# Key tiles of a gated DeltaNet's input in three products of rounded parts, S5 tables spawned one tile later, and a last norm with its sums in three banks

## The chip, the cores and the metric

The kernel runs on one core of a Trainium2 chip. The metric is the device time of one execution in microseconds (us); less is better. All weights lie in HBM in fp32, and every output is fp32.

## The reference, cut to what matters

One inference step of a trunk of four layers, for one prompt of 256 tokens and eight sample sequences of four tokens. Layers 0 and 3 mix with S5, layer 1 with RG-LRU, layer 2 with a gated DeltaNet (gdn); each is followed by a ConvFFN, and one norm ends the trunk. Left out are states, convolutions and the S5 and LRU bodies.

```python
for i in range(DEPTH):
    kind, j = i % N_MIXERS, i // N_MIXERS
    xn = rmsnorm(x, p['norm_mix'][i])
    ...
    x = x + y
    xn = rmsnorm(x, p['norm_ffn'][i])
    y, buf = conv_ffn(xn, ffn_conv[i], ...)
    x = x + y
x = rmsnorm(x, p['norm_final'])

def gdn_mixer(x, s0, conv_buf, w_in, conv_w, a_log, dt_bias, norm_w, w_out):
    proj = x @ w_in
    qkv, z, a_in, b_in = jnp.split(proj, ...)
    qkv, new_buf = causal_dwconv(qkv, conv_buf, conv_w)
    qkv = jax.nn.silu(qkv)
    ...
    beta = jax.nn.sigmoid(b_in)
    g = -jnp.exp(a_log) * jax.nn.softplus(a_in + dt_bias)
    o, s_last = chunked_gated_delta(q, k, v, g, beta, s0)
    o = rmsnorm(o, norm_w) * jax.nn.silu(z)
    return o @ w_out, s_last, new_buf
```

## The kernel before, in words

The 32 sample columns and the 256 prompt columns stand side by side as T = 288 columns of one activation tile `x` (128 partitions x 8 blocks of D = 1024). A projection goes output tile by output tile: `gemm` takes the weight tile of 128 outputs (`wr`, 512 KB, loaded by SP, four buffers) and issues one product of 128x128 weights with 128x288 activations per block of the contraction.

**Two ways of a product.** A weight tile is "whole" (`whole`, line 493) and multiplied in fp32 as it is, `wr` by `xh`; the profile shows two records for each such product. Or it is cut: `wh` is the tile rounded to fp32r (a copy on ACT or DVE), `wl` is the rest, `wr` minus `wh` (DVE or POOL), the activations are cut likewise into `xh` and `xl`, and `part` issues three products, `wh` by `xh`, `wh` by `xl` and `wl` by `xh`. The tiles of the gdn's input (`gdn_in`) are all whole before the change; those of the ConvFFN, the gdn's output and the S5's GLU are cut, with activations `gh` and `gl` there.

**The norm.** A sublayer's projection starts on the `x` that is not yet normed. Meanwhile the squares (`sm`, `acc`) are summed over partitions by products with ones (`busy`), one value for each column in a bank's three columns; twelve short DVE instructions (`nv`, `rsi`, `rst`, `rsr`) make the inverse root, two more a diagonal (`dg`), a product spreads it over all partitions, and DVE copies it from PSUM as `rstd`. Whoever evacuates a tile multiplies by `rstd`.

**Order.** A planner (`Net`) records all instructions at build time. It keeps a clock for each engine with prices and latencies of its own, holds tasks (generators) sorted by rank, and lets a task issue its next instructions when its clock says they are ready; where the TensorE would wait for the operand of a started tile it issues products with `busy` that nobody reads, to keep that engine occupied. The order on each engine is fixed by that, and engines wait for each other by semaphores. So an edit in one stage can move instructions in another.

**The gdn** (`gdn`, line 1529) does 32 tiles of eight products: keys 0 to 7, queries, values, queries, values, then the gates z. `scalars` multiplies the 16 columns of weights for a and b (`wab`) by `xh` and goes on with many short DVE operations to the decay. `ktile` and the like evacuate a tile (`ext`), convolve it (`cv`), apply silu (`kq`) and transpose it on TensorE (`ktm`); `gram`, `rows` and `inverse` build the triangular inverse of each chunk (`fh`, `inv`); `sample`, `update` (`s`), `prompt` and `heads` do the recurrences, with `tm` the normed and gated result of some heads, cut into `gh` and `gl` for the output projection.

**The other places.** `ffn` takes other tasks in `beside`: the tables of the S5 of layer 3 (`s5_tables`, some 200 short DVE instructions, names `er`, `ek`, `dt`, `ang`, `ee`) run beside the ConvFFN of layer 2 (`ffn_down2`). `final` (line 2274) is the last norm: `norm_rstd`, then eight times `y` = x by gain by `rstd` and a store each, with four buffers of `y`.

In the profile every recorded instruction has line 235, that of the planner's helper, and every load or store line 360; so rows are told apart by names. PSUM banks are `ps` and `px`.

Of the kernel before, what the change touches and what calls it, by code (L numbers as in the profile page):

```python
# [9 lines left out]
F32 = mybir.dt.float32  # L10
F32R = mybir.dt.float32r
I32 = mybir.dt.int32
AF = mybir.ActivationFunctionType
ALU = mybir.AluOpType
PSUM = bass.MemoryType.PSUM

P = 128
D = 1024
KD = D // P
NB, NT = 8, 4  # L20
NS = NB * NT
SEQ = 256
T = NS + SEQ
# [3 lines left out]
KL = LW // P  # L27
BLK = (slice(NS, NS + P), slice(NS + P, T), slice(0, P))
EPS = 1e-6
# [6 lines left out]
TR = 0, 0  # L36
HJ = 2
OE, CE = 0, 'a'
PRS, DB, TH, BI = 1, 4, 8, 0.0
SR, SS = (0, 2, 1), (1000.0, 2000.0)  # L40
WHOLE = (0, 4, 6)
WARM = 3500.0


# [248 lines left out]
class Net:  # L293
# [55 lines left out]
    def fresh(self, gi):  # L349

        kinds = (("xh", F32),) if gi in WHOLE else (("xh", F32R), ("xl", F32R)) if gi < 8 else ()
        self.xh, self.xl = ([self.xs.tile([P, KD, T], dt, name=n, tag=n) for n, dt in kinds] + [None, None])[:2]
# [140 lines left out]
    def whole(self, u):  # L493

        name, m = self.units[u][:2]
        return name.startswith(("s5_in", "gdn_in")) or name == "lru_in" and m >= KL

    def freed(self, u):
        return (self.over if self.whole(u) else self.cutl) > u
# [108 lines left out]
    def norm_tile(self, m, gi):  # L608
# [9 lines left out]
        if m == KD - 1:  # L618

            self.last = sq  # L620
            self.mark(("n", gi, m))
        if gi in WHOLE:
            self.mark(("x", gi, m))
        yield
        if gi < 8 and gi not in WHOLE:
            self.v.scalar_tensor_tensor(
# [90 lines left out]
    def ffn(self, li, gi, beside=()):  # L717
        tc, V, G, A = self.tc, self.v, self.g, self.act
        H = 2
        g0 = 2 * li + 1  # L720
        NE = NB * (H + NT) + H + SEQ
        NC = NE - H
        with ExitStack() as es:
            c = es.enter_context(tc.tile_pool(name="ffc", bufs=1))
# [54 lines left out]
            start, name = 2, f"ffn_up{li}"  # L779
            for m, ps in enumerate(self.gemm(name, range(start), KD, self.xh, self.xl, self.xready(g0))):  # L780
                self.spawn(up(m % 2, m // 2, ps))
            for m in range(start, 2 * KF):
                self.spawn(up(m % 2, m // 2, *self.gemm(name, [m], KD, self.xh, self.xl)))
            for g in beside:
                self.spawn(g)
            self.fresh(gi)
            for m in range(KD):
                ready = None if m else (lambda k: self.marked(("d", li, k)))
                self.spawn(self.residual(m, *self.gemm(f"ffn_down{li}", [m], KF, gh, gl, ready), gi))
                if m == 0:  # L790
                    self.dma(self.o["ffn_st"][li], sto)

    def exp_ops(self, p, x, pool, tag):

        V = self.v
        def t(n, dt=F32):
            return pool.tile(list(x.shape), dt, name=n, tag=f"{tag}{n}", bufs=1)
        xc, kf, r, s = t("ex"), t("ek"), t("er"), t("es", I32)
        V.tensor_scalar(xc, x, -87.0, 88.0, op0=ALU.max, op1=ALU.min)
        yield  # L800
        V.tensor_scalar(kf, xc, 1.0 / math.log(2.0), MAGIC + 127.0, op0=ALU.mult, op1=ALU.add)
        yield
        V.tensor_single_scalar(s, kf.bitcast(I32), 23, op=ALU.logical_shift_left)
        V.tensor_scalar_sub(kf, kf, MAGIC + 127.0)
        yield
        V.scalar_tensor_tensor(r, kf, -0.693145751953125, xc, op0=ALU.mult, op1=ALU.add)
        yield
        V.scalar_tensor_tensor(r, kf, -1.42860682030941723e-06, r, op0=ALU.mult, op1=ALU.add)
        yield
        yield from self.horner_ops(p, r, [1.0 / math.factorial(n) for n in range(8, 0, -1)])  # L810
        V.scalar_tensor_tensor(p, p, 1.0, s.bitcast(F32), op0=ALU.add, op1=ALU.mult)
        yield
# [716 lines left out]
    def gdn(self, gi):  # L1529
        tc, V, G, A, PE = self.tc, self.v, self.g, self.act, self.pe  # L1530
        NH, NTL = 8, 16
        H = 3
        g0 = 4
        NE = NB * (H + NT) + H + SEQ
        NC = NE - H
        with ExitStack() as es:
            c = es.enter_context(tc.tile_pool(name="gdc", bufs=1))
            def ct(n, shape, dt=F32):
                return c.tile(shape, dt, name=n)
# [5 lines left out]
            wab, dtp, gnorm = ct("wab", [P, KD, 16]), ct("dtp", [P, 2, NH]), ct("gnorm", [P, 1])  # L1545
# [18 lines left out]
            wh, wl = ct("wh", [P, P], F32R), ct("wl", [P, P], F32R)  # L1564
# [22 lines left out]
            x, xt = (t[:, :512].rearrange("p (t c) -> p t c", t=NTL) for t in inv)  # L1587
# [7 lines left out]
            def pack(dst, src):  # L1595
                for h in range(4):
                    V.tensor_copy(pk[32 * h : 32 * h + 32, dst, :], src[0:32, 2, h::4])

            def scalars():
                yield from self.after("gw")  # L1600
                ps = yield from self.banks.get()
                for k in range(KD):
                    yield from self.after(("x", g0, k))
                    PE.matmul(ps[0:16, :T], wab[:, k, :], self.xh[:, k, :], start=k == 0, stop=k == KD - 1)
                    if k % 2:
                        yield PE
                yield
                t = yield from tms.get()
                self.copy(t[0:16], ps[0:16, :T])
# [2 lines left out]
                ps = yield from self.banks.get()  # L1612
# [41 lines left out]
                ps, pd = yield from self.banks.get(2)  # L1654
# [7 lines left out]
                for h in range(NH):  # L1662
# [4 lines left out]
                        start=True, stop=True, tile_position=(0, 32 * q),  # L1667
# [5 lines left out]
                for hg in range(2):  # L1673
                    V.tensor_scalar(
                        ats[:, hg, :], pd[:, 32 * hg : 32 * hg + 32], pk[:, 0, hg : hg + 1], 0.0,
                        op0=ALU.subtract, op1=ALU.min,
# [554 lines left out]
            start = 2  # L2231
            tiles = self.gdn_order()

            self.spawn(self.norm_rstd(g0))
            self.spawn(scalars())
            self.spawn(sample(0), rank=RK[7])
            self.spawn(sample(1), rank=RK[7])
            fns = ktile, qtile, vtile, ztile
            def rk(m):
                return RK[(0, 0, 1, 3, 2, 4, 5, 5)[m // 4]]  # L2240
            for m, ps in zip(tiles, self.gemm("gdn_in", tiles[:start], KD, self.xh, self.xl, self.xready(g0))):
                self.spawn(fns[m // NH](m % NH, ps), rank=rk(m))
            for m in tiles[start:]:
                self.spawn(fns[m // NH](m % NH, *self.gemm("gdn_in", [m], KD, self.xh, self.xl)), rank=rk(m))
                if m == NH - 1:
                    for r in range(4):
                        self.spawn(gram(r), rank=RK[0])
                    self.spawn(kscalars(), rank=RK[0])
                    self.spawn(rows(), rank=RK[0])
                    self.spawn(inverse(0), rank=RK[0])  # L2250
                    self.spawn(inverse(1), rank=RK[0])
                elif m in (19, 23):
                    self.spawn(prompt((m - 19) // 4), rank=RK[6])
            self.spawn(finals())
            pss = self.gemm("gdn_out", (0, 1), KD, gh, gl, lambda k: self.marked(("gp", k), ("gs", k // 4)))
# [16 lines left out]
            self.ahead()  # L2272

    def final(self):
        self.drain()
        self.spawn(self.norm_rstd(8))
        self.drain()
        yp = self.ctx.enter_context(self.tc.tile_pool(name="yp", bufs=4))
        for m in range(KD):
            y = yp.tile([P, T], F32, name="y", tag="y")  # L2280
            self.v.scalar_tensor_tensor(
                y, self.x[:, m, :], self.gains[:, 8, m : m + 1], self.rstd, op0=ALU.mult, op1=ALU.mult
            )
            self.dma(self.o["y"][:, m, :], y)


def wtiles(w):
# [189 lines left out]
```

## Time and profile before

| | |
|---|---|
| runs | 1572.19, 1572.41, 1567.34 us; median 1572.19 |
| the profiled execution | 1569.18 us, its span 1567.4 us |
| mean granted TensorE clock | 0.98 of full speed |
| TensorE busy | 1503.2 us, 96% of the span |
| VectorE (DVE) busy | 1280.4 us, 82% |
| ScalarE (ACT) busy | 807.0 us, 51% |
| GpSimd (POOL) busy | 360.8 us, 23% |

The span runs from the first to the last instruction of the profiled execution, which is one of its own beside the three runs. Matmuls are pipelined: consecutive records of one stream overlap, so a product's cost is the distance between starts. A row of a timeline gives start, duration, engine, line, operation, out<-in, shapes and count, with the idle time ahead of it and the instruction that ended it in square brackets.

### The profile page before, as it was taken

Reading aid. Unit: us, or ns where it says so; the run is one execution under the profiler, and the core shown is the slowest. Engines: PE = TensorE matmul, PEld = TensorE weight load, DVE = VectorE, ACT = ScalarE, POOL = GpSimd, SP = SyncE. Lnnn points to the kernel's source line nnn. Section 1 sums busy time; section 2 is a strip of 40 time slices with the busy share of each in tenths; the row PEclk is TensorE's granted clock in tenths of the full one; section 3 lists DMA queues with packets and bytes.
Section 4 is the critical chain, followed back from the end, with each engine's and each line's share of the span. In section 5 each row is a group of like instructions: output and inputs, shape, how many; then the busy total and the mean of one; then the engine's idle time right before and its main releaser. Section 6 shows DMA issues by size and latency. Waiting matters only on the chain. (4 is left out here: it accounts for less than half of the span.)

```text
span 1567.4 us, 32702 instructions
## 1 busy us (share of the span) xinstructions
PE 1503.2 (96%) x12527; PEld 1390.6 (89%) x12527; DVE 1280.4 (82%) x2884; ACT 807.0 (51%) x1594; POOL 360.8 (23%) x734
## 2 busy tenths in 40 slices
PE   6689999999999999999999999999999899999996
PEld 5568999999988999998777779999997779999996
DVE  8898799975868899943887677999997967899944
ACT  3475466654574566642543334666444635566631
POOL 2021044520211245400111010444201310245400
PEclk8799999999999999999999999999999999999998
DMA  4422444455425544554322536544545235544552
GB/s 156 113 88 87 161 177 162 163 174 172 174 81 152 195 168 164 163 174 149 122 95 70 195 101 212 178 171 161 156 149 157 55 105 169 166 169 163 161 176 68
DMA packets 84909, 230.05 MB, mean 147 GB/s; under 512 B 19088, under 2 KB 28688, under 8 KB 84752
## 3 DMA queue, kind: packets, MB, share of 16 engines
q1 hardware_dynamic: 84752, 227.96, 44.5%
q8 instruction: 98, 1.61, 0.4%
q14 instruction: 59, 0.48, 0.1%
HBM read 216.94 MB, written 10.99 MB: 145 GB/s over the span
## 5 line engine op out<-in xcount | busy, mean ns | idle before, releaser
L235 DVE TENSOR_TENSOR wl<-wr,wh 128x1024 fp32r<-128x1024 f32 (+2 forms) x338 | 397.9, 1179 | 132.1 <-PE px L235 36.5
L235 ACT ACTIVATE wh<-wr 128x1024 fp32r<-128x1024 f32 (+2 forms) x338 | 344.9, 1023 | 208.2 <-PE ps L235 77.7
L235 DVE SCALAR_TENSOR_TENSOR cv<-ext,par,cv 128x304 f32<-128x304 f32 (+1 forms) x420 | 258.2, 615 | 11.3 <-ACT cv L235 3.3
L235 PE MATMUL px<-xh,wh 128*128 128x288 f32 x776 | 231.0, 298 | 0.0
L235 PE MATMUL px<-xl,wh 128*128 128x288 f32 x776 | 228.9, 295 | 0.0
L235 PE MATMUL px<-xh,wl 128*128 128x288 f32 x776 | 228.7, 295 | 0.0
L235 PE MATMUL ps<-xh,wh 128*128 128x288 f32 x712 | 210.6, 296 | 0.0
L235 PE MATMUL ps<-xl,wh 128*128 128x288 f32 x712 | 210.0, 295 | 0.0
L235 PE MATMUL ps<-xh,wl 128*128 128x288 f32 x712 | 209.9, 295 | 0.0
L235 POOL TENSOR_TENSOR pr<-cv,cv 128x32 f32<-128x32 f32 (+1 forms) x156 | 165.9, 1083 | 58.8 <-DVE cv L235 55.3
L235 POOL COPY sto<-ext 128x16 f32<-128x16 f32 (+3 forms) x379 | 103.4, 275 | 310.8 <-DVE ext L235 287.2
L235 ACT ACTIVATE cv<-ext,par 128x304 f32<-128x304 f32 (+1 forms) x210 | 130.6, 626 | 85.1 <-DVE ext L235 70.7
L235 PE MATMUL ps<-gl,wh 128*128 128x288 f32 x568 | 169.7, 299 | 3.6 <-DVE gl L235 3.3
L235 PE MATMUL ps<-gh,wh 128*128 128x288 f32 x568 | 169.5, 298 | 2.6 <-ACT gh L235 2.5
L235 PE MATMUL ps<-gh,wl 128*128 128x288 f32 x568 | 169.0, 298 | 0.3 <-DVE wl L235 0.3
L235 PE MATMUL px<-gh,wh 128*128 128x288 f32 x536 | 159.1, 297 | 2.4 <-DVE gh L235 2.4
L235 PE MATMUL px<-gh,wl 128*128 128x288 f32 x536 | 158.8, 296 | 0.3 <-DVE wl L235 0.3
L235 PE MATMUL px<-gl,wh 128*128 128x288 f32 x536 | 159.0, 297 | 0.0
L235 PEld LDWEIGHTS px<-xh,wh 128*128 128x128 f32 x776 | 145.9, 188 | 0.8
L235 PEld LDWEIGHTS px<-xl,wh 128*128 128x128 f32 x776 | 145.9, 188 | 0.8
L235 PEld LDWEIGHTS px<-xh,wl 128*128 128x128 f32 x776 | 145.8, 188 | 0.0
L235 PE MATMUL ps<-xh,wr 128*128 128x288 f32 x416 | 125.4, 436 | 12.1 <-DMA wr<-s_in 7.1
(547 smaller groups left out, 3055.0 us busy)
## 6 DMA issues: line engine op xcount, KB each, us to landing
wr<-ffn_up SPq DMA_DIRECT2D x176, 512.0 KB, 3.5
wr<-ffn_down SPq DMA_DIRECT2D x64, 448.0 KB, 3.3
wr<-s_glu SPq DMA_DIRECT2D x32, 512.0 KB, 3.9
wr<-ffn_down SPq DMA_DIRECT2D x32, 512.0 KB, 3.5
wr<-gdn_in SPq DMA_DIRECT2D x32, 512.0 KB, 3.5
wr<-lru_in SPq DMA_DIRECT2D x20, 512.0 KB, 3.2
wr<-s_in SPq DMA_DIRECT2D x16, 512.0 KB, 3.8
wr<-lru_out SPq DMA_DIRECT2D x16, 320.0 KB, 2.9
```

Source lines behind the costliest of these rows:

```text
L235: return f(*a, **k)
```

## The change

**Key tiles.** The first eight tiles of `gdn_in` are no longer whole (`NP3` = 8): their weights are cut and their products are three. The activations of this sublayer therefore come as `xh` and `xl`; the `wab` product is made of three as well, from `wah` and `wal`. For the tiles from 8 on, `operand` writes the fp32 activations `xf` into the buffer that held `xl`, on ACT, eight instructions, once the products of the scalars have been issued.

**Tables.** `beside` is spawned behind the first tile of `ffn_down`, with rank 1 (`RB`) in place of rank 0.

**Last norm.** The sums go into three banks, those of `acc` ahead of the last tile's; 4 and 10 products with `busy` that nobody reads stand behind them (`NK`). Three products of `rsr`, broadcast, with the identity put `rstd` straight into PSUM; `dg` and the copy are gone, `y` is formed from PSUM into one tile, and the stores are five (1, 1, 2, 2 and 2 tiles) in place of eight.

```diff
-WHOLE = (0, 4, 6)
+NK = 4, 10
+WHOLE = (0, 6)
+RB = 1
+NP3 = 8
...
-        return name.startswith(("s5_in", "gdn_in")) or name == "lru_in" and m >= KL
+        return name.startswith("s5_in") or name == "gdn_in" and m >= NP3 or name == "lru_in" and m >= KL
...
-            for g in beside:
-                self.spawn(g)
...
                 if m == 0:
                     self.dma(self.o["ffn_st"][li], sto)
+                    for g in beside:
+                        self.spawn(g, rank=RB)
...
+            def operand(xf):
+                for m in range(KD):
+                    A.activation(xf[:, m, :], self.x[:, m, :], AF.Copy, scale=self.gains[:, g0, m : m + 1])
+                    self.mark(("xf", m))
+                    if m % 2:
+                        yield
...
+                self.copy(wah, wab)
+                V.tensor_tensor(wal, wab, f32(wah), op=ALU.subtract)
...
-                    PE.matmul(ps[0:16, :T], wab[:, k, :], self.xh[:, k, :], start=k == 0, stop=k == KD - 1)
+                    for i, (w, x) in enumerate(((wah, self.xh), (wah, self.xl), (wal, self.xh))):
+                        PE.matmul(ps[0:16, :T], w[:, k, :], x[:, k, :], start=k + i == 0, stop=k == KD - 1 and i == 2)
+                self.mark("gx")
...
             for m in tiles[start:]:
-                self.spawn(fns[m // NH](m % NH, *self.gemm("gdn_in", [m], KD, self.xh, self.xl)), rank=rk(m))
+                if m == NP3:
+                    while not self.marked("gx"):
+                        self.idle()
+                    x2 = self.xs.tile([P, KD, T], F32, name="xf", tag="xl"), None
+                    self.spawn(operand(x2[0]), rank=-1)
+                ready = (lambda k: self.marked(("xf", k))) if m == NP3 else None
+                self.spawn(fns[m // NH](m % NH, *self.gemm("gdn_in", [m], KD, *x2, ready)), rank=rk(m))
...
     def final(self):
-        self.spawn(self.norm_rstd(8))
+            for m in (KD - 2, KD - 1):
+                for ps, b in zip(pss, BLK):
+                    sq = self.acc if m < KD - 1 else self.last
+                    PE.matmul(ps[:, :1], sq[:, b], self.ones[:, :1], start=m < KD - 1, stop=m == KD - 1)
+                for _ in range(NK[m - KD + 2]):
+                    PE.matmul(
+                        spare[:, : 2 * P].rearrange("p (a c) -> p a c", a=2), self.busy,
+                        self.busy.unsqueeze(1).to_broadcast([P, 2, P]), start=True, stop=True,
+                    )
+            for i, ps in enumerate(pss):
+                V.tensor_scalar(v[:, i : i + 1], ps[:, :1], 1.0 / D, EPS, op0=ALU.mult, op1=ALU.add)
+            r = self.rsqrt(v, [P, 3], "nr")
+            for i, b in enumerate((*BLK[:2], slice(0, NS))):
+                PE.matmul(ps[:, b], r[:, i : i + 1].to_broadcast([P, P]), self.ident[:, :n], start=True, stop=True)
...
-                y, self.x[:, m, :], self.gains[:, 8, m : m + 1], self.rstd, op0=ALU.mult, op1=ALU.mult
+                    y[:, m, :], self.x[:, m, :], self.gains[:, 8, m : m + 1], ps[:, :T], op0=ALU.mult, op1=ALU.mult
```

**How instructions move.** DVE at the start of the gdn, from the copy of `rstd` on, before (`tm` and `ab` are the first two steps of the scalars):

```order
L235 COPY rstd<-ps_75 128x288
L235 COPY tm_8425<-px_1686 16x288
L235 TENSOR_TENSOR ab<-px_1687,rsr 128x48
L235 TENSOR_TENSOR t_8406<-ab,dtp 128x24
L235 TENSOR_SCALAR ex<-ab 128x24
```

and DVE at the same place in the changed kernel:

```order
L238 COPY rstd<-ps_75 128x288
L238 TENSOR_TENSOR wl<-wr,wh 128x1024
L238 TENSOR_TENSOR ext_8445<-ps_72,rstd 128x8x4
L238 TENSOR_TENSOR ext_8445<-ps_72,rstd 128x256
L238 TENSOR_TENSOR ext_8446<-px_1685,rstd 128x8x4
L238 TENSOR_TENSOR ext_8446<-px_1685,rstd 128x256
L238 TENSOR_TENSOR wl<-wr,wh 128x1024
L238 COPY tm_8451<-ps_73 16x288
L238 SCALAR_TENSOR_TENSOR cv_8448<-ext_8445,par,cv_8448 128x312 x2
```

The scalars now stand behind two evacuated key tiles and two cuts of weights. Between this copy and `inv<-fh` the whole order has five more `wl`, four fewer `ktm` (they are on ACT now), one fewer `ext` and one more `s<-s,egs` (from POOL).

DVE at the end of layer 2's up projection, before:

```order
L235 TENSOR_SCALAR dt<-er 128x32
L235 SCALAR_TENSOR_TENSOR cv_10713<-ext_10711,par,cv_10713 128x304 x2
L235 TENSOR_TENSOR wl<-wr,wh 128x896
L235 SCALAR_TENSOR_TENSOR dt<-dt,er 128x32 x7
L235 SCALAR_TENSOR_TENSOR dt<-dt,es 128x32
L235 TENSOR_TENSOR gl<-pr_10719,gh 128x288
```

and in the changed kernel:

```order
L238 TENSOR_TENSOR wl<-wr,wh 128x896
L238 TENSOR_TENSOR pr_10905<-cv_10898,cv_10899 128x32
L238 TENSOR_TENSOR pr_10905<-cv_10898,cv_10899 128x256
L238 CAST gh<-pr_10905 128x288
L238 TENSOR_TENSOR gl<-pr_10905,gh 128x288
L238 TENSOR_TENSOR wl<-wr,wh 128x1024
L238 TENSOR_TENSOR x<-x,ps_72 128x288
L238 TENSOR_SCALAR ex<-sc 128x32
```

The tables' first instruction (`ex<-sc`) now stands behind the last `gl` and the first `x`; the last tile's `pr` and `gh`, which were on POOL and ACT, are on DVE.

TensorE in the GLU at the end of layer 3's S5, before:

```order
L235 MATMUL ps_72<-gh,wh 128x288
L235 MATMUL ps_72<-gl,wh 128x288
L235 MATMUL ps_72<-gh,wl 128x288
L235 MATMUL ps_72<-busy 128x224 x10
L235 MATMUL ps_73<-ss_13447,sx 32x72 x8
```

and at the same block of that tile in the changed kernel:

```order
L238 MATMUL px_13931<-gh,wh 128x288
L238 MATMUL px_13931<-gl,wh 128x288
L238 MATMUL px_13931<-gh,wl 128x288
L238 MATMUL px_13931<-busy 128x224
L238 MATMUL ps_74<-gh,wh 128x288
```

Of the 25 idle products in this tail (4, 5, 10 and 6) five are left (4 and 1); the S5's own products stand earlier.

## Rows read from the trace of the kernel before

**Rows 1.** The page: span, busy time of the engines, and one group of instructions.

```profile
span 1567.4 us, 32702 instructions
PE 1503.2 (96%) x12527; PEld 1390.6 (89%) x12527; DVE 1280.4 (82%) x2884; ACT 807.0 (51%) x1594; POOL 360.8 (23%) x734
...
L235 DVE TENSOR_TENSOR wl<-wr,wh 128x1024 fp32r<-128x1024 f32 (+2 forms) x338 | 397.9, 1179 | 132.1 <-PE px L235 36.5
```

**Rows 2.** Waits of PE in 728 to 960 us: total, times, longest.

```profile
PE px L235 <- DVE gh L235: 2.4, 1, 2.4
```

**Rows 3.** Timeline, 738 to 826 us, DVE and PE.

```profile
738.23 0.46 DVE L235 COPY rstd<-ps 128x288 f32<-128x288 f32 x1 [3.11 <-PE ps L235]
...
824.58 1.96 DVE L235 STREAM_TRANSPOSE inv<-fh 128x512 f32<-128x512 f32 x2
...
825.69 0.45 PE L235 MATMUL ps<-inv,fh 32*32 32x32 f32 x32 [1.13 <-DVE inv L235]
```

**Rows 4.** Waits of DVE in 738 to 826 us.

```profile
DVE tm L235 <- PE px L235: 2.4, 1, 2.4
DVE ktm L235 <- PE ps L235: 2.2, 2, 2.0
DVE ab L235 <- PE px L235: 1.4, 1, 1.4
DVE ktm L235 <- PE px L235: 1.3, 1, 1.3
DVE cv L235 <- ACT cv L235: 1.0, 1, 1.0
```

**Rows 5.** Timeline of PE, fp32 products of the gdn's start.

```profile
734.13 1.14 PE L235 MATMUL px<-xh,wab 128*16 128x288 f32 x4
...
774.13 5.02 PE L235 MATMUL px<-xh,wr 128*128 128x288 f32 x20
778.98 0.38 PE L235 MATMUL ps<-ident,kq 128*128 128x128 f32 x2
```

**Rows 6.** Window: busy us (count) of PE, PEld, DVE, ACT, POOL; clock, DMA, GB/s.

```profile
825.70:937.10 111.40, 111.11 (x1286) 82.72 (x1286) 82.92 (x233) 44.89 (x144) 10.14 (x21) 1.00 0.37 124
```

**Rows 7.** Timeline of PE at the start of ffn_down2.

```profile
1118.00 0.29 PE L235 MATMUL ps<-gh,wh 128*128 128x288 f32 x1
...
1118.40 0.29 PE L235 MATMUL ps<-gh,wh 128*128 128x288 f32 x1
...
1120.36 0.40 PE L235 MATMUL ps<-gh,wh 128*128 128x288 f32 x1 [0.90 <-ACT gh L235]
1121.66 0.40 PE L235 MATMUL ps<-gl,wh 128*128 128x288 f32 x1 [0.90 <-DVE gl L235]
```

**Rows 8.** Groups of PE in 1279.5 to 1299.6 us, and one window inside.

```profile
L235 PE MATMUL ps<-busy 128*128 128x224 f32 x25 | 4.3, 319 | 0.0
L235 PE MATMUL ps<-gh,wh 128*128 128x288 f32 x12 | 4.2, 353 | 1.6 <-ACT gh L235 1.6
...
1289.60:1292.10 2.50, 2.36 (x9) 2.15 (x10) 2.35 (x4) 0.00 (x0) 0.01 (x1) 0.63 0.00 0
```

**Rows 9.** Timeline of the end of the program.

```profile
1553.23 0.38 PE L235 MATMUL px<-busy,sm 128*128 128x1 f32 x2 [0.97 <-ACT sm L235]
...
1554.54 0.16 DVE L235 TENSOR_SCALAR nv<-px 128x3 f32<-128x3 f32 x1 [1.90 <-PE px L235]
...
1556.91 0.42 DVE L235 TENSOR_TENSOR dg<-ident,rsr 128x256 f32<-128x256 f32 x1
...
1557.54 1.33 PE L235 MATMUL ps<-dg,busy 128*128 128x288 f32 x2 [3.04 <-DVE dg L235]
...
1559.48 1.80 DVE L235 SCALAR_TENSOR_TENSOR y<-x,gains,rstd 128x288 f32<-128x288 f32 x4
...
1561.92 2.03 DVE L235 SCALAR_TENSOR_TENSOR y<-x,gains,rstd 128x288 f32<-128x288 f32 x4 [0.64 <-DMA o_y<-y]
```

**Rows 10.** Timeline of DVE in layer 3's S5, an operand in PSUM.

```profile
1197.50 0.66 DVE L235 TENSOR_TENSOR u<-ps,rstd 128x288 f32<-128x288 f32 x1
```

More of the change, by code (lines that the diff above doesn't have):

```diff
@@ L1597, in pack @@
                     V.tensor_copy(pk[32 * h : 32 * h + 32, dst, :], src[0:32, 2, h::4])
+            def operand(xf):
[4 more added lines that the diff above has]
+                        yield
+                self.mark("xf")
             def scalars():
                 yield from self.after("gw")
+                wah, wal = (w.rearrange("p (k c) -> p k c", k=KD) for w in (wh, wl))
+                self.copy(wah, wab)
+                yield
+                V.tensor_tensor(wal, wab, f32(wah), op=ALU.subtract)
+                yield
                 ps = yield from self.banks.get()
@@ L2242, in gdn @@
                 self.spawn(fns[m // NH](m % NH, ps), rank=rk(m))
+            x2 = self.xh, self.xl
             for m in tiles[start:]:
-                self.spawn(fns[m // NH](m % NH, *self.gemm("gdn_in", [m], KD, self.xh, self.xl)), rank=rk(m))
+                if m == NP3:
[5 more added lines that the diff above has]
+                self.spawn(fns[m // NH](m % NH, *self.gemm("gdn_in", [m], KD, *x2, ready)), rank=rk(m))
                 if m == NH - 1:
@@ L2274, in final, with norm @@
     def final(self):
-        self.drain()
-        self.spawn(self.norm_rstd(8))
[L2277 to L2281, printed above, removed]
-                y, self.x[:, m, :], self.gains[:, 8, m : m + 1], self.rstd, op0=ALU.mult, op1=ALU.mult
-            )
-            self.dma(self.o["y"][:, m, :], y)
+        V, PE = self.v, self.pe
+        y = self.xs.tile([P, KD, T], F32, name="y", tag="xh")
+        def norm():
+            yield from self.after(("n", 8, KD - 2))
+            pss = yield from self.banks.get(3)
+            spare = yield from self.banks.get()
+            for m in (KD - 2, KD - 1):
+                yield from self.after(("n", 8, m))
+                for ps, b in zip(pss, BLK):
[6 more added lines that the diff above has]
+                    )
+            v = self.work.tile([P, 3], F32, name="nv", tag="nv")
+            for i, ps in enumerate(pss):
+                V.tensor_scalar(v[:, i : i + 1], ps[:, :1], 1.0 / D, EPS, op0=ALU.mult, op1=ALU.add)
+            r = self.rsqrt(v, [P, 3], "nr")
+            ps = pss[0]
+            for i, b in enumerate((*BLK[:2], slice(0, NS))):
+                n = b.stop - b.start
+                PE.matmul(ps[:, b], r[:, i : i + 1].to_broadcast([P, P]), self.ident[:, :n], start=True, stop=True)
+            e = 0
+            for m in range(KD):
+                V.scalar_tensor_tensor(
+                    y[:, m, :], self.x[:, m, :], self.gains[:, 8, m : m + 1], ps[:, :T], op0=ALU.mult, op1=ALU.mult
+                )
+                if m not in (2, 4, 6):
+                    self.dma(self.o["y"][:, e : m + 1, :], y[:, e : m + 1, :])
+                    e = m + 1
+        self.spawn(norm())
+        self.drain()
 def wtiles(w):
```

## The prediction, made before the changed kernel had run

> **What bounds the kernel now.** I read the page first: TensorE is busy for 1503.2 of 1567.4 us, 96%, and DVE for 1280.4 [rows 1]. So whatever lengthens or shortens TensorE's stream moves the end, unless DVE takes the bound over for a while. Then I read the waits and the timelines of the four places that the change touches. In the gdn, TensorE runs without a pause from its start to 825.69 us, where it waits 1.13 us for `inv` from DVE [rows 3]. From there to the end of the input projection it is busy for 111.11 of 111.40 us while DVE has 82.92 [rows 6]; behind that it waits 2.4 us for `gh` [rows 2]. That 1.13 us wait, short as it is, says the most: up to `inv` TensorE and DVE end nearly together, so a gain on TensorE counts there only as far as DVE gets shorter too. DVE's stretch runs from the copy of `rstd` at 738.23 to the transposes of 824.58 to 826.5 [rows 3]. In it DVE itself waited 2.4 us for `tm`, 1.4 for `ab`, 3.5 for `ktm` and 1.0 for `cv` [rows 4], 8.3 together; the other 79.2 of its 87.5 us are work and the short gaps between instructions.
>
> **Key tiles, TensorE's side.** Ten fp32 products take 778.98 less 774.13, 0.485 each [rows 5]. Three products of rounded parts take 0.40, from 1118.00 to 1118.40 [rows 7]. The eight key tiles have 64 such products: 64 x 0.085 = 5.4 less. Of the scalars two fp32 products took 1.14 [rows 5], so eight take 4.6; 24 of rounded parts at 0.133 take 3.2, 1.4 less. The order adds five idle products there, at the mean distance of the others in a stream some 0.13 each: 0.7 more. TensorE's work up to `inv` falls by 6.1 us.
>
> The Trainium skill (FP8 and Floating Point Precision, section TensorE Precision Notes) has fp32 in four passes, so three products of rounded parts would save a quarter of 31.0 us, 7.8; the rows show 0.40 against 0.485, a saving of 18%, and the sum goes by the rows.
>
> **Key tiles, DVE's side.** The sums of the norm come behind eight triples (3.2 us) where they came behind four fp32 products (1.9): `rstd` is 1.3 later. Up to `inv` the order adds five `wl` at 1.18 [rows 1], 5.9, and one `s<-s,egs`, a 128x1024 product like `wl`, 1.2; it takes away four `ktm` of 128x256 and an `ext`, which I put at 0.4 each, near the 0.42 of `dg` of the same size [rows 9], 2.0. That is 5.1 more. In return `tm` and `ab` now stand behind evacuations and cuts that are ready before them, and `ktm` leaves DVE, so I let 7.3 us of its waits go and keep the 1.0 for `cv`. `inv` is then at 825.7 + 1.3 + 5.1 - 7.3 = 824.8: **0.9 us less**, although TensorE could be there 7.2 earlier (6.1 and its wait of 1.13). It will wait some 6 us there instead, in one piece or in several. Bounds: -7.2 if DVE's gaps shrink as well, +6.4 if all waits stay.
>
> From `inv` on, TensorE has no slack and both orders hold the same products, so the shift is carried to the tail. The tail's wait for `gh` hangs on DVE's last recurrences and `z`; the order has the same operations there, the last `z` four updates of `s` earlier and `tm` directly behind them. I leave it at nothing; if its cover is wrong, the ends are the 2.4 us that would go [rows 2] and as much again.
>
> **xf.** It is written into `xl`'s buffer, so the first ACT instruction has to wait until the last key product has read `xl`. Eight products on `kq` stand between that product and the first with `xf`, and products of the sample's states between the next ones, which covers it; without the cover the nearest row is 0.90, the wait for ACT at the next sublayer's start [rows 7]. I take 0, with ends 0 and 1.5. The eight more `wh` are on ACT, which is busy for 51% of the span.
>
> **Tables one tile later.** Before, 11 table instructions stood on DVE behind the cut of the weights and ahead of the last `gl`, for which TensorE waited 0.90, and 0.90 for `gh` before it [rows 7]. Now none is ahead of them, and `pr` and `gh` of that tile have moved to DVE, which gives part of it back. One of the two waits goes: **-0.9**, ends -1.8 and 0. The tables end later by about a tile; the order has their last instruction still ahead of the last `x` of ffn_down2, and DVE idles there now, so nothing is late.
>
> **The S5's tail.** This is no part of the edit but follows from the planner's new clock. There are 25 idle products, 4.3 us of records or about 3.4 in starts, a wait of 1.6 us for `gh` [rows 8], and behind it a window at 0.63 of the clock, where nine products took 2.4 in place of 1.2. The order keeps 5 of the 25. A planner that no longer fills does not make `gh` earlier, so I take half of what fillers fall by: **-1.8**, ends -5.2 (fillers and wait gone) and +2 (waits in place of fillers, with twice that window's loss).
>
> **The last norm.** Three sums instead of six behind `sm`, at 0.22 each: -0.66; three `nv` in place of one: +0.4. No `dg` (1556.91 to 1557.54): -0.63 [rows 9]. The product of 1.33 at 1557.54 and the copy up to 1559.48 take 1.94 [rows 9]; three products of 288 columns in all stay, which I put between 1.33 and half of it, at 1.0, with 0.1 until DVE goes on: -0.84. The eight `y` lose the 0.64 us wait for a store's buffer [rows 9]. The last store is twice as long, put at +0.5, ends 0 and 1. Sum: -0.66 + 0.4 - 0.63 - 0.84 - 0.64 + 0.5 = -1.9, **-1.9** with ends -2.7 and -0.9.
>
> **Sum.** -0.9 - 0.9 - 1.8 - 1.9 = -5.5 us. The profiled execution took 1569.18, so one like it would take 1563.7. It lies 3.0 us below the median of the runs, 1572.19, by which it would be 1566.7; the runs themselves spread over 5 us. I take the middle, **1565.2 us**. What a measurement can tell from no change is 0.3%, 4.7 us: faster means under 1567.5, slower above 1576.9.
>
> **Rivals.**
> *A, TensorE sets the gdn's end (chance 0.16).* If DVE's gaps shrink with its queue fuller, the stage gains 7.2 in place of 0.9: 1565.2 - 6.3 = 1558.9. For it: 132.1 us of idle time ahead of `wl` in the whole kernel show that DVE can take more [rows 1]. Against: this stretch has under a tenth of its time in waits [rows 4].
> *B, the gains of the gdn and the S5's tail are only in the order (0.20).* Then the waits of DVE and the real time of `gh` stay, and only tables and norm count: -2.8, which is 1567.9, no change.
> *C, DVE becomes the gdn's bound outright (0.10).* The cuts of the keys join a queue whose waits do not go: `inv` at 825.7 + 6.4. TensorE, 6.1 shorter, then stands still for over 12 us in all, and after such waits its clock is lower for a time (0.63 in the S5's tail after 1.6 us [rows 8], a loss of 1.2). The stage costs 7.6 more; with tables, tail and norm at -4.6 that is +3.0: 1573.7, slower in sign; with the S5's tail at +2 too it is 1577.5. It decides from the point where `inv` lies more than 4.6 us later than 825.7.
> *D, `y` from PSUM is slow (0.06).* One operand in PSUM and one in SBUF took 0.66 [rows 10] where four `y` from SBUF took 1.80, 0.45 each [rows 9]: eight times 0.2, 1.7 lost, 1566.9. Against it: the copy of `rstd` from PSUM, of as many elements, took 0.46 [rows 3]. The Trainium skill (VectorE: DVE Perf Modes, section Rules for kernel authors) advises to copy a matmul's output to SBUF first if many operations read it, and eight do here.
>
> **How the numbers follow.** The forecast has 0.48. Within its terms' ends it lies under 1567.5 about five times in six (0.40). With A (0.16), most of D (0.04) and a quarter of B (0.05), faster has 0.65. Slower has half of C and a little of the forecast's upper ends, 0.07; 0.28 is left for no change. The range reaches from somewhat under A, 1557.5, to between B and C, 1571.5; outside lie most of C and A's best ends, under 2 in 10. The forecast's own range is 1561 to 1569.
>
> **What would show it.** Right: key products at 0.40 per triple; DVE without the waits for `tm`, `ab` and `ktm`; a wait of several us in all on TensorE ahead of `inv`, and `inv` within 2 us of 825. No wait for `gl` or `gh` over 0.9 at ffn_down2's start. In the S5's tail, fewer idle products but a longer wait for `gh`. From the last `sm` to the first `y` 4.5 us where it was 6.25 [rows 9], and no wait between the `y`. Wrong: `inv` at 819 (A) or after 830 (C), an S5 tail as long as before (B), or `y` at 0.65 each (D).

## The result, and the profile after

The changed kernel ran at 1549.57, 1554.17, 1553.71 and 1551.56 us, median 1552.63, against a median of 1572.26 in four runs of the kernel before: the ratio is 0.988, with a 95% interval of 0.9855 to 0.9906. It is 19.6 us faster where 7 were forecast, and lies under the range of 1557.5 to 1571.5. Four later runs of the same kernel on another chip (e13 below) had a median 14.8 us under that of the kernel before (0.9902, 0.9885 to 0.9918), so the size of the gain is known to some five us only. The profiled execution took 1549.57 us, its span 1547.7, 19.7 less than before [rows 1].

The table gives both profiled executions stage by stage. A stage runs from the start of its first product in TensorE's timeline to that of the next; the gdn's input is parted at the first product on `inv`, and the last stage runs from the end of the last projection's products to the end of the span.

| stage | before | after | difference | forecast |
|---|---|---|---|---|
| start to layer 1's output projection | 482.27 | 481.97 | -0.3 | 0 |
| layer 1's output projection | 35.28 | 34.50 | -0.8 | 0 |
| up1, down1 (ConvFFN of layer 1) | 211.27 | 211.27 | 0.0 | 0 |
| gdn input up to `inv` | 96.87 | 91.29 | -5.6 | -0.9 |
| gdn input from `inv` on | 111.40 | 109.68 | -1.7 | 0 |
| gdn output projection | 32.32 | 30.59 | -1.7 | 0 |
| up2 | 141.45 | 141.46 | 0.0 | 0 |
| down2 | 74.04 | 70.58 | -3.5 | -0.9 |
| S5 of layer 3 with its GLU | 155.81 | 152.74 | -3.1 | -1.8 |
| up3, down3 | 211.43 | 211.77 | +0.3 | 0 |
| last norm | 15.26 | 11.80 | -3.5 | -1.9 |

So each of the four forecast terms has its sign, but all were too small, the gdn's most: 9.0 us came out of its three rows, not 0.9.

The page of the changed kernel, span and engines, to be read against [rows 1]:

```profile
span 1547.7 us, 32882 instructions
PE 1488.2 (96%) x12602; PEld 1387.6 (90%) x12602; DVE 1293.2 (84%) x2906; ACT 814.1 (53%) x1600; POOL 351.0 (23%) x726
```

TensorE has 15.0 us less to do, DVE 12.8 more. Its timeline in the gdn, DVE and PE, which answers to [rows 3]:

```profile
737.05 0.46 DVE L238 COPY rstd<-ps 128x288 f32<-128x288 f32 x1 [1.68 <-PE ps L238]
...
817.89 1.99 DVE L238 STREAM_TRANSPOSE inv<-fh 128x512 f32<-128x512 f32 x2
...
819.03 0.45 PE L238 MATMUL ps<-inv,fh 32*32 32x32 f32 x32 [0.43 <-DVE inv L238]
```

The stretch of DVE from the copy of `rstd` to the end of the transposes is 82.8 us (737.05 to 819.88) where it was 88.3. The waits of DVE in 738 to 826 us, which answer to [rows 4]:

```profile
DVE mt L238 <- ACT at L238: 1.4, 3, 0.8
DVE cv L238 <- ACT cv L238: 0.6, 2, 0.4
DVE wl L238 <- ACT cv L238: 0.4, 1, 0.4
```

No wait for a product of TensorE is left among them. The waits of TensorE from the gdn's start to the first product on `inv` (727.8 to 819.5 us):

```profile
PE px L238 <- ACT kq L238: 1.2, 1, 1.2
PE ps L238 <- ACT tm L238: 0.8, 1, 0.8
PE ps L238 <- DVE inv L238: 0.4, 1, 0.4
```

That is 2.4 us in all where it was 1.5; the prediction had some 6 for `inv`. The waits of TensorE in ffn_down2 (1100.7 to 1171.5 us), which answer to the two of 0.90 in [rows 7]:

```profile
PE px L238 <- DVE wl L238: 0.5, 1, 0.5
```

Windows over ffn_down2, the S5's input and body, and its GLU, before and then after (busy us of PE, PEld, DVE, ACT, POOL with counts; clock, DMA share, GB/s):

```profile
1110.86:1185.06 74.20, 72.40 (x532) 71.76 (x531) 67.35 (x211) 28.87 (x41) 4.11 (x7) 0.98 0.52 157
1185.06:1270.09 85.03, 77.42 (x944) 60.09 (x942) 70.75 (x152) 50.49 (x118) 18.93 (x30) 0.96 0.34 97
1270.09:1340.87 70.78, 68.14 (x733) 64.61 (x732) 51.29 (x79) 30.97 (x53) 3.99 (x12) 0.98 0.44 146
```

```profile
1100.76:1171.50 70.74, 70.23 (x531) 70.00 (x530) 67.99 (x213) 28.43 (x40) 4.20 (x6) 1.00 0.55 165
1171.50:1253.38 81.88, 72.55 (x831) 56.37 (x830) 66.83 (x146) 47.47 (x113) 10.35 (x27) 0.96 0.38 112
1253.38:1324.24 70.86, 67.95 (x825) 64.11 (x824) 55.51 (x89) 33.34 (x59) 5.43 (x12) 1.00 0.43 133
```

The GLU is as long as before, with 92 more records in it and 20 of the idle products gone, while the S5's body ahead of it has 113 records less and is 3.2 us shorter. The timelines name what moved: 112 records of the S5's own products (`sx`, `sx,tt` and `ss,ca`), 4.2 us in starts, left the body; the same number came into the GLU, where they take 3.8 and the idle products 3.2 less. So work of the S5 now stands where the idle products stood. The end of the program, which answers to [rows 9]:

```profile
1536.94 0.61 PE L238 MATMUL ps<-busy,sm 128*128 128x1 f32 x4
1537.36 0.38 DVE L238 TENSOR_SCALAR nv<-ps 128x1 f32<-128x1 f32 x2 [1.01 <-PE ps L238]
...
1540.19 0.85 PE L238 MATMUL ps<-ident,rsr 128*128 128x128 f32 x6 [1.12 <-DVE rsr L238]
1541.08 3.49 DVE L238 SCALAR_TENSOR_TENSOR y<-x,gains,ps 128x288 f32<-128x288 f32 x8 [0.95 <-PE ps L238]
```

From the first sum of `sm` to the first `y` it takes 4.14 us (1536.94 to 1541.08) in place of 6.25, the eight `y` 3.49 in place of 4.47, and from the last `y` to the end 3.1 in place of 3.5.

### The profile page after: what moved, and what is told of

The parts are those of the page before. It is cut to its first block, busy times and chain, and to the rows that moved or that the text cites. A ratio compares the mean times of both kernels' runs of the same rounds, so it can differ in the third digit from the quotient of the medians.

```text
span 1547.7 us, 32882 instructions
## 1 busy us (share of the span) xinstructions
PE 1488.2 (96%) x12602; PEld 1387.6 (90%) x12602; DVE 1293.2 (84%) x2906; ACT 814.1 (53%) x1600; POOL 351.0 (23%) x726
## 5 line engine op out<-in xcount | busy, mean ns | idle before, releaser
L238 DVE TENSOR_TENSOR wl<-wr,wh 128x1024 fp32r<-128x1024 f32 (+2 forms) x346 | 407.8, 1180 | 131.1 <-PE px L238 38.2
L238 ACT ACTIVATE wh<-wr 128x1024 fp32r<-128x1024 f32 (+2 forms) x346 | 353.4, 1024 | 220.7 <-PE px L238 84.7
L238 PE MATMUL px<-xh,wh 128*128 128x288 f32 x816 | 243.5, 298 | 0.0
L238 PE MATMUL px<-xl,wh 128*128 128x288 f32 x816 | 240.7, 295 | 0.0
L238 PE MATMUL px<-xh,wl 128*128 128x288 f32 x816 | 240.5, 295 | 0.0
L238 PE MATMUL ps<-xh,wh 128*128 128x288 f32 x744 | 219.9, 296 | 0.0
L238 PE MATMUL ps<-xl,wh 128*128 128x288 f32 x744 | 219.5, 295 | 0.0
L238 PE MATMUL ps<-xh,wl 128*128 128x288 f32 x744 | 219.3, 295 | 0.0
L238 POOL COPY sto<-ext 128x16 f32<-128x16 f32 (+2 forms) x374 | 100.1, 269 | 322.8 <-DVE ext L238 299.5
L238 PEld LDWEIGHTS ps<-xl,wh 128*128 128x128 f32 x744 | 139.1, 187 | 0.7
```

What stands on the lines that cost most here:

```text
L238: return f(*a, **k)
```

## The experiments

**One part alone, three runs.** Each is the kernel before with the lines of one part of the diff.

```diff
-WHOLE = (0, 4, 6)
+WHOLE = (0, 6)
+NP3 = 8
...
```

stands for e1, with the lines of `whole`, `operand`, `scalars` and the loop over tiles;

```diff
-            for g in beside:
-                self.spawn(g)
...
+                    for g in beside:
+                        self.spawn(g, rank=RB)
```

is all of e2, and e3 has the new `final`.

> Only the key tiles and the scalars in three products; tables and last norm as before. Theory A (TensorE sets the length of the gdn; the three parts add up): the gdn input 7.3 us shorter and its output projection 1.7, as in the changed kernel, ffn_down2 and the end as before; 1572.3 less 9, less 0 to 1.5 in the S5's tail, whose order has 11 idle products here in place of 25: 1562 to 1563.5. Theory F (the forecast's: DVE is the bound up to inv and gives back only 0.9): 1571, and the gain in the changed kernel's gdn came from somewhere else.

> Only the tables one tile later. Theory A: both waits at the start of ffn_down2 go (1.8 us) and with them the stretch at half the clock that follows (1.7): 3.5 less; the S5's tail keeps 17 idle products of 25, 1 less: 1567.8. Rival (the waits alone, the clock falls anyway or the tables are late for the S5): 1 to 2 less, 1570.5, or none.

> Only the last norm. From the last sm to the end 3.4 us shorter, as in the changed kernel (2.1 up to the first y, 1.0 in the eight y, 0.3 in the last store): 1568.9. Rival (the gain at the end was shared with another part, or the runs' spread): 1 to 2 us, 1570.5.

Measured on one chip, the kernel before at a median of 1570.72 us: keys 1559.22 (ratio 0.9925, 0.9901 to 0.9948), tables 1568.06 (0.9985, 0.9974 to 0.9996), norm 1568.71 (0.9982, 0.9969 to 0.9994). That is 11.5, 2.7 and 2.0 us less, 16.2 in all, where the whole change gave 14.8 to 19.6 on two chips; the runs' own spread leaves some us open. The stages say it more sharply, since a stage of the same order comes out within 0.1 us in most executions (the first stage, layer 1's output projection, the S5's body and the old last norm do not). With the keys alone the gdn is 91.21, 109.60 and 30.60 us, 9.2 less, all that the whole change has there. With the tables alone down2 is 70.44. With the norm alone the last stage is 11.81, 3.4 less, the whole of it; but with the old order this stage took 14.6 to 15.5 us in five profiles, mostly by the time from the last `y` to the end, so the gain is 2.8 to 3.7. Down2 took 72.8 us in four other executions with the old order (e1, e3 and two below) and 74.04 only in the profile of before, so that the tables' own gain is 2.3, and 1.2 of the 3.5 was that execution. The S5 of layer 3 got shorter with the keys alone (153.2 us) and with the tables alone (154.3), with its own code unchanged; in the changed kernel's two profiles it took 152.7 and 154.6, so its gain is known to some 2 us only.

**Which engine sets the way up to `inv`, three runs.** Work that nobody needs is put into the key tiles past the planner, so that the rest of the order stays: 16 additions on DVE, in the changed kernel (e4) and in the one before (e6), and 48 idle products on TensorE in the changed kernel (e5).

```diff
             def ktile(h, ps):
                 yield from conv(h, ps, kq[:, h, 0, :])
+                for _ in range(2):
+                    self.tc.nc.vector.tensor_tensor(self.acc, self.x[:, 0, :], self.x[:, 1, :], op=ALU.add)
...
                 ps = yield from self.banks.get()
+                for _ in range(6):
+                    self.tc.nc.tensor.matmul(ps[:, :P], self.busy, self.busy, start=True, stop=True)
```

> The changed kernel with 16 more DVE additions of 128x288 (two for each key tile, about 0.37 us each, 6 us in all) that the planner does not know of, so that the rest of the order stays; they write the buffer of the sum of squares, which nobody reads then. Theory A with DVE slack (TensorE alone sets the stage): inv within 1 us of 819.0, time as the changed kernel's, 1552.6. Theory B (DVE and TensorE end together at inv, TensorE waits for it 0.4 us now): inv about 5 us later, gdn input 5 longer, 1557.5.

> The changed kernel with 48 more idle products of 128x128 on TensorE (six for each key tile, ahead of its transposes, some 0.06 to 0.1 us each, 3 to 5 us in all) that the planner does not know of. Theory B1 (DVE alone decides when inv is ready): TensorE has time to spare, the stretch up to inv stays within 1 us of 91.3. Theory B2 (DVE itself runs at the pace of TensorE's tiles, so both decide): 3 to 5 us longer.

> The kernel before with the same 16 DVE additions in its key tiles (5.9 us) as were put into the changed kernel. Theory F (forecast: DVE's stretch decides inv before, its waits do not give): up to inv 5 to 6 us longer, 102.5. Theory B2 (before, DVE waits for products, 10 us in all, and these waits take the additions in): up to inv less than 3 longer, 97 to 100.

The first product on `inv` in each of the three, from the timeline:

```profile
828.82 0.45 PE L238 MATMUL ps<-inv,fh 32*32 32x32 f32 x32
```

```profile
823.58 0.45 PE L238 MATMUL ps<-inv,fh 32*32 32x32 f32 x32 [0.43 <-DVE inv L238]
```

```profile
828.49 0.45 PE L235 MATMUL ps<-inv,fh 32*32 32x32 f32 x32 [1.15 <-DVE inv L235]
```

The gdn began at 731.81, 727.99 and 728.55 us in them, so the way up to `inv` was 97.01 us in e4, 95.59 in e5 and 99.94 in e6. The additions take 7.0 us in starts (0.44 each, not the 0.37 that was expected), the idle products 5.7 (0.12 each). In the changed kernel the additions cost 5.7 us and the idle products 4.3, about four fifths and three quarters of what they take: both engines are nearly full there, and theory B2 holds. TensorE's idle products also show whom DVE waits for: its waits in the stretch grew from 1.8 to 5.6 us in e5, most of it in two waits for TensorE that the changed kernel does not have (DVE's waits in e5, 737.8 to 824.4 us):

```profile
DVE wl L238 <- PE ps L238: 1.7, 1, 1.7
DVE ext L238 <- PE ps L238: 1.5, 1, 1.5
```

In the kernel before the same additions cost 3.1 us, less than half: its DVE had room, and its waits fell from 10.3 to 7.4 us. Those for `ktm` fell from 3.5 to 0.9 and the one for `ext` (0.6) went; those for `tm` and `ab`, which stand ahead of the additions, stayed as in [rows 4] (DVE's waits in e6):

```profile
DVE tm L235 <- PE px L235: 2.4, 1, 2.4
DVE ab L235 <- PE px L235: 1.4, 1, 1.4
DVE ktm L235 <- PE px L235: 0.5, 1, 0.5
DVE ktm L235 <- PE ps L235: 0.4, 1, 0.4
```

Idle products on TensorE in the kernel before, the fourth of these trials, were not run. The medians, with one round, were 1557.72 (e4), 1555.17 (e5) and 1570.74 us (e6, the kernel before at 1571.03); that e6's median is not 3 us higher lies within the spread of the runs.

**Idle products in the S5 (e7).** The kernel before without the 25 idle products of the S5 of layer 3; the planner still counts their time.

```diff
+            if self.used > self.mute:
+                self.pe.real = SimpleNamespace(matmul=lambda *a, **k: None)
             self.pe.matmul(
...
             )
+            self.pe.real = real
```

> The kernel before without the 25 idle products in layer 3's S5, order and all else unchanged. Theory G (gh is there when they are issued, they cost what they take): the stretch from the start of that S5's input to the end of its GLU, 155.8 us before, 3 to 4 shorter, and that was the gain of the changed kernel. Theory W (gh and gl come when they come): waits take the place of the idle products, the stretch stays within 1 us, or gets longer by some us where the clock falls in the waits; then the changed kernel's gain there comes from the earlier gh, by the moved order.

Median 1573.85 us against 1571.03. The S5 with its GLU took 158.4 us, in place of 155.8 in the profile of before and of 157.3 and 156.9 in e3 and e6; the GLU alone was 73.0, not 70.6, at this clock:

```profile
1271.75:1344.78 73.03, 67.37 (x707) 63.46 (x705) 51.37 (x79) 31.08 (x52) 3.99 (x12) 0.91 0.45 140
```

So theory W holds: the idle products, 4.0 us in starts, stand in time that TensorE would mostly wait anyway (its waits in the GLU grew from 2.5 to 5.7 us), and without them its clock falls (0.91, before 0.98). The changed kernel therefore gains nothing by their absence as such; what fits is the useful products in their place.

**More and fewer cut tiles, three runs.** e8 cuts the eight z tiles as well, with `xl` made anew on DVE; e11 cuts the first four queries too; e15 cuts six key tiles only.

```diff
-name == "gdn_in" and m >= NP3
+name == "gdn_in" and NP3 <= m < 24     (e8)
+name == "gdn_in" and m >= 12           (e11)
+name == "gdn_in" and m >= 6            (e15)
```

> The changed kernel with the eight z tiles in three products too: their xl is made anew on DVE in the buffer of xf. By theory B2, behind inv TensorE alone is the limit (109.7 us, DVE under 92 of them): 64 products at about 0.1 to 0.17 less, 6 to 11 us, less 33 idle products that the planner now puts at the tail (4) and less what eight more wl (9.4 us) and eight xl (4) do to DVE's dense tail: 1552.6 less 0 to 6. Rival (DVE's tail becomes the bound): 0 to 6 longer.

> The changed kernel with twelve tiles in three products, the keys and the first four queries. Theory B2 (up to inv DVE and TensorE are both full): 32 products are 0.1 us each shorter, 3.3 less on TensorE, but four wl of 1.18 come onto DVE, 4.7: up to inv 1 to 5 us longer than 91.3, in all 1552.6 plus 0 to 5. Rival (TensorE alone, the forecast's case A): 2 to 3 us shorter up to inv.

> The changed kernel with six key tiles in three products in place of eight. Theory B2 (TensorE and DVE are both full up to inv with eight tiles, TensorE alone with none): 16 products cost 0.1 us each more on TensorE, 1.6; two wl less on DVE, which gives nothing back as TensorE sets the pace again: 1 to 2.5 us more up to inv. Rival (DVE is the tighter of the two with eight tiles): up to 1 us less up to inv.

Medians: 1559.41 (e8), 1565.24 (e11), 1560.86 us (e15), all above those with eight (1552.63 and 1554.97); for e8 the intervals of the ratios overlap, and its stages decide. With the z tiles the part behind `inv` is 108.84 us, only 0.8 shorter where 6 to 11 were expected, and the output projection behind it 37.64, 7.1 longer: TensorE now waits 5.4 us behind `inv`, nearly all for DVE, so the rival is the nearer, and DVE's tail takes more than TensorE gives. With twelve tiles the way up to `inv` is 94.15, 2.9 longer, as theory B2 has it, with 7.6 us of TensorE's waits in it. But the part behind it is 5.6 longer and the output projection 3.4, and the whole 12.6, far outside the 0 to 5 that were expected. With six it is 96.51, 5.2 longer, which neither theory had, and the part behind `inv` is 113.60, 3.9 longer. The first of these can be parted: the fp32 products up to `inv` take 46.7 us in starts where they took 35.0, being 90 in place of 68, while the cut ones give back 6.1. Of the 22 more, 16 are the two key tiles; six are products that stood behind `inv` with eight tiles, some 3.1 us of the 5.2. So with six tiles only 0.4 us of the gain up to `inv` is left, and the larger part of the loss is the planner's other order and not the work of the two tiles. The gain is no smooth function of the number, and for eight tiles order and work were not tried apart.

**The last norm, two runs.** e9 copies `rstd` to SBUF and forms `y` from there; e10 has no idle products.

```diff
+            rstd = self.work.tile([P, T], F32, name="rstd", tag="rstd")
+            V.tensor_copy(rstd, ps[:, :T])                       (e9)
-NK = 4, 10
+NK = 0, 0                                                       (e10)
```

> The changed kernel with rstd copied from PSUM to SBUF and y formed from there, as before. Theory: the y from PSUM cost no more than those from SBUF (eight took 3.49 us), so the copy comes on top, 0.5 us from the last product to the end of the span more than the changed kernel's 11.85. Rival D (an operand in PSUM is slower, 0.2 us each): 0.5 added and up to 1.6 gained, 1 us less.

> The changed kernel without the 14 idle products of the last norm. Theory (they keep the clock up for the last three products and cost nothing): the products with the identity take 1.3 to 1.7 us at half the clock in place of 0.85, 0.5 to 0.8 more up to the end. Rival (the four ahead of the sums are in the way): 0.2 to 0.4 less.

The last stage took 12.34 us in e9 and 12.45 in e10, in place of 11.80, with medians of 1554.97 and 1554.78 us. In e9 the timeline has the copy, and eight `y` from SBUF as long as those from PSUM:

```profile
1544.99 0.46 DVE L238 COPY rstd<-ps 128x288 f32<-128x288 f32 x1 [0.95 <-PE ps L238]
1545.48 3.52 DVE L238 SCALAR_TENSOR_TENSOR y<-x,gains,rstd 128x288 f32<-128x288 f32 x8
```

In e10 the last products take 1.49 us in place of 0.85, at a granted clock of 0.50, after TensorE has stood for 2.4 us:

```profile
1543.68 1.49 PE L238 MATMUL ps<-ident,rsr 128*128 128x128 f32 x6 [2.42 <-DVE rsr L238]
```

Both as the theories had it, and rival D is out.

**The clock in layer 1's output projection, three runs.** This stage has the same order in all kernels so far, but took 34.5 us in the changed kernel's profile, 37.9 to 38.5 in seven others and 37.0 and 37.3 in e8 and e9. e12 and e14 put four and two idle products ahead of each of three products that wait there; e13 is the changed kernel again.

```diff
+        if late is not None and nk == KL and n >= nk - 3:
+            for _ in range(4):
+                self.tc.nc.tensor.matmul(
+                    late[:, T:].rearrange("p (a c) -> p a c", a=2), self.busy,
+                    self.busy[:, : 256 - T // 2].unsqueeze(1).to_broadcast([P, 2, 256 - T // 2]), start=False, stop=False,
+                )
```

> The changed kernel with three times four idle products in the first tile of layer 1's output projection, where TensorE waits for gh and gl; that stage took 34.5 us at a clock of 1.00 in the changed kernel's profile and 38 at 0.91 in others of the same order. Theory: the clock falls in some executions behind these waits, the idle products prevent it, at no cost as they stand in the waits: 34.5 to 35 us there in the profile, the runs near 1550 with a smaller spread. Rival (they delay the waiting products, or the clock falls all the same): 0 to 1.5 us longer.

> The changed kernel once more, beside the two below on the same chip. The stages from the gdn's input on as in its first profile within 0.1 us each (the S5's within 1.5); layer 1's output projection at 34.5 to 38 us, by whether the clock falls there. 1549.5 to 1554.5, median 1552.6.

> The changed kernel with three times two idle products in the first tile of layer 1's output projection, half of the earlier trial. Theory: that is enough to keep the clock at 1.00 there and delays less: 34.5 to 35.3 us for the stage, 1 to 2 us under the changed kernel's median on the same chip. Rival: with two the clock falls in some executions (38 us), no difference in the median.

e12 had a median of 1551.99 us; in another set of runs e13 had 1554.97 (1552.34 to 1556.66) and e14 1551.62 (1549.75 to 1552.62). The stage was 36.08, 36.06 and 35.90 us in their profiles, so the 34.5 to 35.3 expected of e12 and e14 was missed by about one. e13 lies just outside its own expectation too, and its S5 is 1.9 us longer than in the first profile, while its gdn stages agree within 0.1. In e12 and e14 the wait for `gl` was there, 1.56 and 1.55 us, and the granted clock stayed 1.00; in the nine profiles with a wait of 1.4 to 1.6 us and no such products it was 0.91 or 0.95. So the idle products did hold the clock in two profiles of two, and what is left above 34.5 is the wait itself, 0.3 us in the profiles of 34.5; why it is longer in some executions is open. In e13 that wait was 0.28, yet the clock fell for a time (0.95). That e14 lies 3.3 us under e13 in four runs each is a hint; of the 4.0 us between their profiles 1.8 lie in the first stage and 2.1 in the S5, where they do not differ in code, so the cause is not settled. e14 is the fastest version seen beside the changed kernel of the same chip, 0.9878 of the kernel before (0.9861 to 0.9894) against 0.9902 (0.9885 to 0.9918).

## Why the prediction was wrong

**The step that failed.** It is the sum of DVE's side. The prediction saw that TensorE and DVE end nearly together at `inv`, which is true, and let TensorE's gain of 6.1 us count only as far as DVE got shorter. By its sum that was 0.9, so TensorE would stand for some 6 us. DVE's end came 5.6 us earlier, and TensorE waited 2.4 in all up to `inv`, 0.4 of it for `inv`, where it had waited 1.5. TensorE's own account closes: 6.4 us less of products up to `inv` and 0.9 more of waits, with no fp32 product moved across `inv`. Behind the sum stands the reading of DVE's stretch as full. It was 88.3 us long (the prediction wrote 87.5) and held 10.3 us of waits (it listed 8.3), 9.3 of them for TensorE's products. e6 shows that such a stretch has room: more than half of what was added to DVE vanished there. e5 shows that DVE's waits follow TensorE: they grew by 3.8 when it got 5.7 more to do. Only in the changed kernel are both nearly full (e4, e5). That more room lay in the faster products than in the changed order is not shown: e15 has six of the eight cut tiles and another order, and nearly none of the gain.

Case A, with 0.16, was the nearest. Its 7.2 us stood for the way up to `inv`, where 5.6 came. That the whole input is 7.3 shorter agrees by luck, since 1.1 of the 1.7 behind `inv` are products that moved on into the output projection; so is `inv` at 819.0, A's own sign, as the gdn itself began 1.1 us earlier.

**The terms of DVE's side.** It was to end 0.9 earlier; it ended 5.6 earlier, counted from the gdn's start. All three terms were off, all one way, by 1.4, 1.1 and 2.1. `rstd` was to be 1.3 later: it came 9.31 us after the gdn's start in place of 9.41; the sums come behind more products, yet DVE had waited for its product anyway (3.11 us ahead of the copy before, [rows 3], 1.68 now). Of the waits 7.3 were to go: 8.4 went (10.3 to 1.8, in the stretch itself). Of work 5.1 was to be added: counted by starts and without waits it is 81.0 us in place of 78.0, 3.0 more. What was priced came near, 4.7 more (five `wl` 5.7, `s` 1.2, less 1.7 for `ktm` and 0.4 for `ext`). The 1.8 less lie in instructions that no term has. The largest that both the changed kernel and e1 show is 1.0: two small instructions of the scalars, `t` and `beta`, which overlap, took 1.19 and 1.10 us before, beside a memset of POOL of 1.06, and 0.18 and 0.17 now. Why the rest differs is open.

**TensorE's side.** The key products were priced at 0.085 us of saving each, from a stream of fp32 products (0.485). In the stage as it is, broken up by other products, the fp32 products took 133.0 us in starts for 256, 0.52 each; the 64 of the keys took 32.8, 0.51 each, and the cut ones 25.9 for 64 triples, 0.405: 6.9 us less for the keys, not 5.4. The other fp32 products up to `inv` took 0.5 more. The scalars gave 0.9, not 1.4, the idle products cost 0.9, not 0.7. Together that is 6.4 less up to `inv`, so TensorE's sum of 6.1 was right within 0.3, by errors that cancel. Behind `inv` the stage is 1.7 shorter and the output projection 1.7, both put at nothing. Eight records of products `vm,kts`, 1.07 us, moved from the first to the second, which is most of the first gain and a loss for the second; against it the second gained 1.1 in the wait for `gh` (2.4, now 1.3) and 1.4 in its own products, which took 27.3 us in starts before, some of them at the lower clock (0.5 to 0.6 for some 4 us behind the wait, 1.00 throughout now), and 26.0 now.

**Tables.** The mechanism was right and the size off: both waits went, not one (one of 0.5 for `wl` stands later in the stage, where the old order had 0.2 in most executions), and in the profile of before the clock had fallen behind them, with products 0.24 us apart, in place of 0.13, from 1122.95 to 1126.2. With the 72.8 us of the other executions the term is -2.3 in place of -0.9.

**The S5's tail.** The sign was right, the place not. It was said that fewer idle products make the tail shorter by half their time; e7 shows that they cost nothing. The GLU kept its length and the body ahead of it became 3.2 us shorter. The timelines show 4.2 us of the body's products moved into the GLU, against which the body's waits grew by 1.7; that this move alone makes the gain was not tried by itself.

**The last norm.** -3.5 for -1.9. Up to the first `y` 2.1 were gained where the terms sum to 1.7, mostly since three products took 0.9 and the clock stayed up, which e10 shows to be worth 0.6; the `y` gained 1.0 where 0.64 was counted; and from the last `y` to the end, where the larger last store was put at +0.5, it took 3.1 us in every profile with the new order and 2.8 to 3.7 with the old, so that term is not settled.

**The rest.** The rivals B, C and D did not come: B's waits of DVE went, C's `inv` was early, D's `y` were as fast. The Trainium skill (FP8 and Floating Point Precision, section TensorE Precision Notes) has fp32 in four passes, and the estimate by it was 7.8 us for the keys. With 6.9 measured in the stage, 21% of the fp32 products' time, neither that quarter nor the 18% of the rows was met, and the stream of fp32 products alone still shows 0.485.

## What to carry to other kernels

Before a second engine is called the bound of a stretch, part its time into work and waits, and ask what each wait is for: waits for the engine that gets faster can shrink with it. Work slipped in past the planner, once on each engine, tells in two runs which of them has room. Where a planner orders the instructions, look at what it moved before a gain or a loss is put down to the work: with six tiles in place of eight the order took away more than the work. And price an instruction by its distance to the next one in the stage where it stands, not in the cleanest stream of its kind.

## What was not expected of the hardware

Layer 1's output projection took 34.5 us in four profiles of the same order, 37.9 to 38.5 in seven, and 35.3 to 37.3 in four more. In the seven TensorE waits 1.4 to 1.6 us for `gl` where it waits 0.3 in the four, and behind that wait the clock falls to half. In e3, whose wait was 1.42 us, it stayed there for some seven us (windows of e3):

```profile
486.00:490.00 4.00, 2.77 (x11) 1.92 (x12) 3.52 (x11) 1.71 (x3) 0.00 (x0) 0.77 0.50 164
490.00:494.00 4.00, 4.00 (x18) 4.00 (x18) 1.19 (x2) 1.67 (x4) 0.00 (x0) 0.50 0.60 163
494.00:498.00 4.00, 4.00 (x29) 4.00 (x28) 2.45 (x4) 1.57 (x3) 0.00 (x0) 0.88 0.31 86
```

With the profile of before at 35.28 and ffn_down2 there at 74.0 or 72.8, two such places move an execution of this kernel by up to 5 us, which is as much as the spread of its runs and more than two of the three parts of the change gave. The stages ahead of this one add to it: they took 481.6 to 485.7 us in the seventeen profiles.
